# 80 instead of 64 gathered tokens, U products of 304 columns, and half scores and the last modulation in the step list of a transformer block with product-key experts

## The chip, the cores and the metric

The kernel runs on one core of a Trainium2 chip. The metric is device time in microseconds (us) of one execution, without compiling and without moving the inputs in; the median of three runs of the kernel before is 1428.74 us.

The engines named below: PE multiplies matrices (its weight loads are shown as PEld), DVE and ACT work on vectors, POOL does some vector work and issues gathers, SP issues most other transfers. Each engine takes its own instructions in the order in which they were written to its queue; semaphores hold one back until what it needs is there.

## The reference

512 tokens of width 1024 go through two mixers side by side (attention with a window of 128, and gated linear attention), an output projection, and then a layer of 16,384 experts. Each token picks, for each of 8 heads, 16 experts; an expert is one row of `u` and one row of `v`.

```python
def peer_ffn(h, wq, subkeys, u, v):
    q = (h @ wq).reshape(B, S, PEER_HEADS, 2, PEER_QDIM // 2)
    sub_scores = jnp.einsum('bshpk,hpnk->bshpn', q, subkeys)      # 2 x 128 scores a head
    top_v, top_i = lax.top_k(sub_scores, 16)
    cand = top_v[..., 0, :, None] + top_v[..., 1, None, :]        # 256 candidates
    cand_i = top_i[..., 0, :, None] * 128 + top_i[..., 1, None, :]
    best_v, best_pos = lax.top_k(cand, 16)
    expert = jnp.take_along_axis(cand_i, best_pos, axis=-1)
    gates = jax.nn.softmax(best_v, axis=-1)
    # per token, over its 8 x 16 experts:
    hid = gelu(einsum('tkd,td->tk', u[expert], h)) * gates
    return einsum('tk,tkd->td', hid, v[expert])

mod = silu(c) @ w_ada + b_ada                   # six vectors of 1024
shift1, scale1, gate1, shift2, scale2, gate2 = split(mod)
h = rms_norm(x, norm1_w) * (1 + scale1) + shift1
x = x + gate1 * (concat([attention(h), gla(h)]) @ w_out)
h2 = rms_norm(x, norm2_w) * (1 + scale2) + shift2
x = x + gate2 * peer_ffn(h2, wq, subkeys, u, v)
return rms_norm(x, final_norm_w)
```

## The kernel before

All products of 32-bit numbers are made of three matmuls on a high and a low part (`mm3`, L97 to L100); the high part is a copy by ACT (L91), the low one a subtraction, mostly by DVE (L92). The tokens stand in four blocks of 128.

**Front (0 to about 262 us).** Modulation, first norm, mixers, output projection, second norm. The work is written as generators, one step at a time; the list `parts` holds them, and the table `ORDER` (L49 to L66) names at each place the generator that makes its next step. All five engines follow this order by hand. `query_load` and `query_part` at its end make the query products of heads 0 and 1, in halves of 256 tokens. Vectors 3 and 4 of the modulation are steps of the list too.

**Query stage (262 to 396 us).** `wq_head(h)` (L1281) for h = 0 to 7: for h > 1 the query products (512 columns), then the scores `pss` of each pair of blocks (L1303), their copy by ACT, and on DVE the search for the 16 best of 128 by `max`, `max_index` and `match_replace` (L1314 to L1318). After heads 3 and 7 `candidates` (L1260) does the second search. Here also stands vector 5 of the modulation (`mod_part(5)` at h = 4; eight operations `macc` on DVE, L258 and L260) and the first chunks of the next stage as filler.

**Routing stage (396 to 732 us).** Two strands. One, on PE: the products `ph` of chunks of 128 experts' rows of u with h2 of the first 320 tokens (24 matmuls of 320 columns a chunk, `u_matmuls`, L1222), with a split of the chunk on ACT and DVE ahead and a GELU (L1229) behind; 86 of the 128 chunks are done here (`AHEAD`), the rest in the next stage. A chunk's split waits for the GELU of the chunk four earlier (`issue_after(gelus[-4])` in `u_part`). The other strand, on DVE above all: the routing itself (`route_heads`, `route`), then for 384 tokens, 16 at a time, the one-hot matrices that turn the gates into a dense table (`one_hot`, `gate_group`, L1450, L1468, L1471, with matmuls `pg` at L1483).

**The gathered tokens.** For the last 64 of these 384 tokens nothing is multiplied densely in U: their h2 is laid out in two copies on the partitions (`sp_rows`), their experts' numbers and gates are moved so that a partition holds one token's half (`sp_index`, L1541), and then POOL gathers 64 times 128 rows of u (`sp_gather`, L1562, 512 KB each) and DVE forms 128 dot products at a time (`sp_dot`, L1568). The rows turn through buffers: the first 20 (`HEAD`) through 7, the others through 3. Dot m frees its buffer and gather m + 3 is issued after it. `woven` places the 44 rows after the head among 51 pieces of the one-hot work. `sp_finish` applies GELU and `sp_close` multiplies by the gates and moves the result back.

What stands where on DVE and POOL is set by a planner: it sums DVE and PE work by a table of costs and takes the next U chunk when PE has fallen behind its share (`DVE_ALL`, `PE_ALL`). This stage holds a manual schedule on DVE and POOL, so the order that the planner writes is the order of execution.

**V stage (740 to 1402 us).** For 128 chunks: the dense table of gates times the GELU, times the rows of v, in `acc` (18 matmuls of 512 columns a chunk), with the 42 U chunks that are left between them; beside it POOL and DVE treat the fourth block's 128 tokens by gathered rows of u and v (`gather_u`, `gather_v`, L1618 to L1658). After it the final norm and the stores, to 1425.8.

Of the kernel before, what the change touches and what calls it, by code (L numbers as in the profile page):

```python
# [2156 lines left out]
```

## Time and profile before

| what | us |
|---|---|
| median of three runs (1428.49 to 1429.4) | 1428.74 |
| the profiled execution, its own time | 1427.61 |
| its span in the profile | 1425.8 |
| PE busy in the span | 1387.3 (97%) |
| DVE busy in the span | 1264.4 (89%) |
| ACT, POOL busy | 658.8, 608.2 |
| HBM read and written | 395.52 MB and 42.47 MB |

A page row gives for each engine its busy time and its number of instructions. The slices are the span in 40 equal parts, a digit the tenths in which an engine was busy. A window row gives busy times of the engines between two moments. A group row is one line of the code with one shape: how often, busy time, mean of one in ns, and the idle time ahead of them with what ended it. `his` and `los` are the high and low parts, `spr` the gathered rows, `spix` and `spg` their numbers and gates, `qsc` scores, `best` the results of a search, `macc` a sum of the modulation, `o` one-hot matrices.

### The profile page before, as it was taken

The numbers are of one execution on the slowest core, as the hardware profiler recorded it, in microseconds if no ns is written. First come the engines' busy times: TensorE is split into PE (matmuls) and PEld (weight loads), VectorE is DVE, ScalarE is ACT, GpSimd is POOL, SyncE is SP. The second block draws the span as 40 slices with busy tenths as digits, with TensorE's granted clock in tenths as the row PEclk, the third lists the DMA queues.
The fourth block names the chain that finished last, engine by engine and source line by source line (L and its number), as shares of the span: only waits on it lengthen the run. The fifth ranks groups of instructions, "written<-read, shape, count | busy, mean of one in ns | idle before, by whom it ended". The sixth has DMA issues, their size and how long they took to land.

```text
span 1425.8 us, 23257 instructions
## 1 busy us (share of the span) xinstructions
PE 1387.3 (97%) x8788; PEld 1224.4 (86%) x8788; DVE 1264.4 (89%) x2314; ACT 658.8 (46%) x1113; POOL 608.2 (43%) x400
## 2 busy tenths in 40 slices
PE   5999999999999999999989999999999999999997
PEld 4777788987999999999989888888888888888885
DVE  7778887599999999999978899999898998998986
ACT  4458565532444576666854333333333333333333
POOL 2000000334606444233145676767676776555510
PEclk9999999999999999999999999999999999999999
DMA  9621553352359999999889999999999999999962
GB/s 356 255 89 60 177 209 142 115 218 90 126 194 383 353 338 364 329 340 344 307 324 414 413 413 411 411 413 410 402 406 396 397 376 413 399 414 408 414 240 74
DMA packets 127873, 439.62 MB, mean 308 GB/s; under 512 B 11888, under 2 KB 48528, under 8 KB 107408
## 3 DMA queue, kind: packets, MB, share of 16 engines
q1 hardware_dynamic: 69024, 252.21, 46.4%
q0 software_dynamic: 47136, 171.99, 30.8%
q10 hardware_dynamic: 11600, 13.93, 2.7%
q8 instruction: 69, 1.13, 0.3%
q14 instruction: 44, 0.36, 0.1%
HBM read 395.52 MB, written 42.47 MB: 307 GB/s over the span
## 4 chain that ended last, share of the span: by engine, by line
PE 65%; DVE 6%; issue 6%; POOL 3%; DMA 1%; ACT 1%; ACTq 0%; POOLq 0%; DVEq 0%
PE acc L98 12%; PE acc L100 12%; PE acc L99 12%; PE ph L100 8%; PE ph L98 8%; PE ph L99 8%; POOL spr L1562 3%; PE pg L1483 2%; DMA spr<-in_u_dram,spix 1%; PE pq L99 1%; DVE macc L260 1%; PE pq L100 1%; PE pq L98 1%; DVE best L1315 1%; DVE qsc L1316 1%
## 5 line engine op out<-in xcount | busy, mean ns | idle before, releaser
L98 PE MATMUL ph<-h2Th,his 128*128 128x320 f32 x1024 | 319.7, 312 | 2.4 <-ACT his L1923 1.9
L100 PE MATMUL ph<-h2Th,los 128*128 128x320 f32 x1024 | 316.0, 310 | 2.5 <-DVE los L1930 1.8
L99 PE MATMUL ph<-h2Tl,his 128*128 128x320 f32 x1024 | 315.8, 308 | 0.0
L1618 POOL DMA_INDIRECT gu<-in_u_dram,ix_u x128 | 214.4, 1675 | 148.0 <-DVE gu L1628 82.4
L1653 POOL DMA_INDIRECT gv<-in_vP_dram,ix_v x128 | 210.5, 1644 | 111.9 <-DVE gacc L1658 86.9
L98 PEld LDWEIGHTS ph<-h2Th,his 128*128 128x128 f32 x1024 | 192.6, 188 | 4.3 <-ACT his L1923 2.1
L100 PEld LDWEIGHTS ph<-h2Th,los 128*128 128x128 f32 x1024 | 192.3, 188 | 3.5 <-DVE los L1930 2.0
L99 PEld LDWEIGHTS ph<-h2Tl,his 128*128 128x128 f32 x1024 | 192.7, 188 | 0.8
L1562 POOL DMA_INDIRECT spr<-in_u_dram,spix x64 | 104.8, 1637 | 170.9 <-DVE spr L1568 128.5
L98 PE MATMUL acc<-his,Ah 128*128 128x512 f32 x432 | 168.0, 389 | 0.0
L99 PE MATMUL acc<-los,Ah 128*128 128x512 f32 x432 | 168.0, 389 | 0.0
L100 PE MATMUL acc<-his,Al 128*128 128x512 f32 x432 | 168.0, 389 | 0.0
L1658 DVE SCALAR_TENSOR_TENSOR gacc<-gv,hg,gacc 128x1024 f32<-128x1024 f32 x127 | 162.5, 1280 | 3.2 <-DMA gv<-in_vP_dram,ix_v 3.0
L1628 DVE SCALAR_TENSOR_TENSOR gu<-gu,h2n 128x1024 f32<-128x1024 f32 x128 | 155.5, 1218 | 4.4 <-DMA gu<-in_u_dram,ix_u 4.4
L98 PE MATMUL acc<-hi,Ah 128*128 128x512 f32 x336 | 131.3, 391 | 0.0
L100 PE MATMUL acc<-hi,Al 128*128 128x512 f32 x336 | 131.1, 390 | 0.0
L99 PE MATMUL acc<-lo,Ah 128*128 128x512 f32 x336 | 130.7, 389 | 0.0
L1926 ACT ACTIVATE Ah<-gr 128x768 fp32r<-128x768 f32 x64 | 53.5, 836 | 139.8 <-PE acc L99 128.5
L91 ACT ACTIVATE his<-u 128x1024 fp32r<-128x1024 f32 x86 | 90.4, 1054 | 26.3 <-PE pq L99 11.6
L92 DVE TENSOR_TENSOR los<-u,his 128x1024 fp32r<-128x1024 f32 x75 | 91.2, 1218 | 5.5 <-ACT his L91 5.5
L98 PEld LDWEIGHTS acc<-his,Ah 128*128 128x128 f32 x432 | 81.1, 188 | 16.9
L100 PEld LDWEIGHTS acc<-his,Al 128*128 128x128 f32 x432 | 81.1, 188 | 16.8
(708 smaller groups left out, 2863.7 us busy)
## 6 DMA issues: line engine op xcount, KB each, us to landing
u<-in_uT_dram SPq DMA_DIRECT2D x43, 1024.0 KB, 7.5
gr<-Gd SPq DMA_DIRECT2D x15, 1536.0 KB, 11.1
Gd<-gs SPq DMA_DIRECT2D x10, 2048.0 KB, 10.0
gsp<-ge ACTq DMA_DIRECT2D x40, 320.0 KB, 6.4
wa<-in_w_ada_dram SPq DMA_DIRECT2D x12, 1024.0 KB, 5.3
wq<-in_wq_dram SPq DMA_DIRECT2D x8, 1024.0 KB, 5.7
gp<-gsp SPq DMA_DIRECT2D x22, 320.0 KB, 9.5
gp<-gsp SPq DMA_DIRECT2D x36, 160.0 KB, 9.6
```

The source lines that it names most:

```text
L91: nc.scalar.activation(hi, src, AF.Copy)
L92: lo_eng.tensor_tensor(lo, src, hi, OP.subtract)
L98: nc.tensor.matmul(acc, lh, rh, start=start, stop=False)
L99: nc.tensor.matmul(acc, lh, rl, start=False, stop=False)
L100: return nc.tensor.matmul(acc, ll, rh, start=False, stop=stop)
L1483: nc.tensor.matmul(pt[:, i, :], o12[:, g, 0, :, r], o2[:, g, m, :, r], start=(m == 0), stop=(m == 2))
L1562: nc.gpsimd.indirect_dma_start(out=sp[m], out_offset=None, in_=a["u"], in_offset=bass.IndirectOffsetOnAxis(ap=sp["ix", i][:, j:j + 1], axi ...
L1618: nc.gpsimd.indirect_dma_start(out=ur, out_offset=None, in_=a["u"], in_offset=bass.IndirectOffsetOnAxis(ap=ix_u[:, s:s + 1], axis=0))
L1628: nc.vector.scalar_tensor_tensor(ur, ur, 1.0, h2n, op0=OP.mult, op1=OP.mult, accum_out=hid[:, s:s + 1])
L1653: nc.gpsimd.indirect_dma_start(out=vr, out_offset=None, in_=a["vP"], in_offset=bass.IndirectOffsetOnAxis(ap=ix_v[:, s:s + 1], axis=0))
L1658: nc.vector.scalar_tensor_tensor(gacc, vr, hg[:, s:s + 1], gacc, op0=OP.mult, op1=OP.add)
L1926: nc.scalar.activation(grp(Ah), A, AF.Copy)
```

## The change

- `SETS` gets a second set: 16 tokens ahead of the 64. 80 tokens are gathered and dotted (80 rows instead of 64, the first set's rows with 8 copies of 16 tokens on the partitions), and the dense U products have 304 columns instead of 320.
- Two more groups in `ODD_AHEAD`, with two chunks each: 90 chunks are done in the routing stage instead of 86, and 38 in the V stage instead of 42.
- `woven` may take more than one row at a place (`while` for `if`), so 60 rows after the head stand at the same 51 places. The first set is finished in the first block of the one-hot work, the second where the one set was.
- `sp_index` and `sp_close` move each set with one transfer a copy: 8 of 16x16 for the first, 2 of 64x64 for the second.
- Vector 5 of the modulation is a generator of the step list; `query_part(h)` there makes the products of the first 256 tokens alone and their scores (`pssa`). `first_heads` then does, in an order by hand, the other 256 tokens' products of heads 0 and 1, their scores and the searches; `wq_head` serves h from 2 to 7. The two U chunks that stood after head 1 move to the others.
- `ORDER` is another table throughout (its other lines are left out below).

```diff
--- before.py
+++ after.py
...
-SETS = ((TD - 64, 64),)
+SETS = ((TD - 80, 16), (TD - 64, 64))
 TS = sum(n for c, n in SETS)
...
-ODD_AHEAD = tuple(range(21, 32))
+ODD_AHEAD = tuple(range(19, 32))
 KEPT = 3
...
ORDER = """
-2 2 2 2 2 0 0 0 0 2 0 2 0 0 0 2 25 25 0 0 2 13 0 13 13 25 25 25 13 0 1 1 1 1 2 1 13 1 1 25 25 2 13 25 1 2 13 25
...
+2 2 2 2 2 13 13 13 2 0 2 13 0 0 0 0 0 2 0 13 25 25 2 66 0 13 2 25 13 0 2 13 13 25 2 13 0 0 25 3 25 25 25 0 1 22
...
-                acc = Eg[:, 2 * v - 2:2 * v, :].rearrange("p a b -> p (a b)")
+                at = 4 if v == 3 else 6
+                acc = Eg[:, at:at + 2, :].rearrange("p a b -> p (a b)")
...
-    def query_part(h, half):
+    early = {}
+
+    def query_products(h, half):
         ts = slice(half * 256, half * 256 + 256)
         for s in range(2):
             for k in range(KD):
-                tag = "ph" if h == 0 else "m"
                 yield
-                if half == k == 0:
-                    query_banks[h, s] = pbank(f"pq{h}{s}") if h == 0 else bank(f"pq{h}{s}")
+                if half == s == k == 0:
+                    query_banks[h] = [pbank(f"pq{h}{i}") if h == 0 else bank(f"pq{h}{i}") for i in range(2)]
                 hh, ll = (t[:, s * P:(s + 1) * P] for t in queries[h, k])
-                mm3(query_banks[h, s][:, ts], hh, ll, h2Th[:, k, ts], h2Tl[:, k, ts], k == 0, k == KD - 1)
+                mm3(query_banks[h][s][:, ts], hh, ll, h2Th[:, k, ts], h2Tl[:, k, ts], k == 0, k == KD - 1)
+
+    def score_products(pt, qh, sk):
+        pt = pt.rearrange("p (a b c) -> p a b c", a=2, b=2)
+        for i in range(2):
+            for s in range(2):
+                nc.tensor.matmul(pt[:, i, s, :], qh[:, s, i * P:(i + 1) * P], sk[:, s, :], start=True, stop=True)
+
+    def query_part(h):
+        steps = query_products(h, 0)
+        next(steps)
+        for i in range(2 * KD):
+            yield
+            next(steps, None)
+        yield
+        if "q" not in early:
+            early["q"] = frW.tile([P, 2, 2, 256], F32, tag="h2_0", bufs=1, name="qh_")
+        for s in range(2):
+            nc.scalar.activation(early["q"][:, h, s], query_banks[h][s][:, :256], AF.Copy)
+        yield
+        if h == 0:
+            early["two"] = bank2("pssa")
+        score_products(early["two"][:, h], early["q"][:, h], early["sk", h])
...
-                 + [query_load(0), query_load(1)] + [query_part(h, half) for h in range(2) for half in range(2)]
-                 + [modulation(3), modulation(4)] + [attention_parts(n) for n in ALL])
+                 + [query_load(0), query_load(1)] + [query_part(h) for h in range(2)]
+                 + [modulation(3), modulation(4)] + [attention_parts(n) for n in ALL] + [modulation(5)])
...
+    def first_heads():
+        copy = lambda t, src: nc.scalar.activation(t, src, AF.Copy)
+        place = lambda pair: sca[:, pair].rearrange("p a b c -> p (a b c)")
+        for h in range(2):
+            nc.sync.dma_start(SKR[h], a["skT"][:, 2 * h:2 * h + 2, :])
+        rest = [query_products(h, 1) for h in range(2)]
+        for g in rest:
+            next(g)
+        run = lambda h, n: [next(rest[h], None) for _ in range(n)]
+        two = early.pop("two")
+        copy(place(0), two[:, 0])
+        copy(place(1), two[:, 1])
+        del two
+        run(0, 2 * KD)
+        search(0, 0, 0)
+        for s in range(2):
+            copy(qha[:, 0, s, 256:], query_banks[0][s][:, 256:])
+        run(1, KD)
+        two = bank2("pssb")
+        score_products(two[:, 0], qha[:, 0, :, 256:], SKR[0])
+        search(1, 0, 1)
+        copy(place(0), two[:, 0])
+        run(1, KD)
+        search(0, 1, 0)
+        for s in range(2):
+            copy(qha[:, 1, s, 256:], query_banks[1][s][:, 256:])
+        query_banks.clear()
+        return two
...
     def wq_head(h):
-        if h > 1:
-            w = load_group(a["wq"][h], h, 256, "wq", (nc.gpsimd, nc.gpsimd))
+        w = load_group(a["wq"][h], h, 256, "wq", (nc.gpsimd, nc.gpsimd))
...
-        for n0 in range(0, NT, 2):
-            pt = two[:, n0 // 2].rearrange("p (a b c) -> p a b c", a=2, b=2)
...
-                if h % 4 == 3:
+        for pair in range(2):
+            score_products(two[:, pair], qh[:, :, pair * 256:pair * 256 + 256], sk)
+            nc.scalar.activation(sca[:, pair].rearrange("p a b c -> p (a b c)"), two[:, pair], AF.Copy)
+            search(h, pair, pair)
+            if h % 4 == 3:
+                for n in range(2 * pair, 2 * pair + 2):
...
-        for src, key, dt in ((sp["e"], "ix", I32), (gates[SB], "g", F32)):
-            if i == 0:
-                for r in range(P // n):
-                    nc.sync.dma_start(sp[key, i][r * n:(r + 1) * n], src[s0:s0 + n, r * n:(r + 1) * n])
-            else:
-                d = dr.tile([P // n, n, n], dt, name=f"d{key}{i}")
-                nc.sync.dma_start(d.rearrange("r t j -> t r j"), src[s0:s0 + n].rearrange("t (r j) -> t r j", j=n))
-                nc.sync.dma_start(sp[key, i], d.rearrange("r t j -> (r t) j"))
+        for src, key in ((sp["e"], "ix"), (gates[SB], "g")):
+            for r in range(P // n):
+                nc.sync.dma_start(sp[key, i][r * n:(r + 1) * n], src[s0:s0 + n, r * n:(r + 1) * n])
...
+    engines = {mybir.EngineType.PE, mybir.EngineType.Activation, mybir.EngineType.DVE}
+    with tc.manual_schedule(engines=engines):
+        two = first_heads()
+    fetch(a["wq"][2], 2, 256, "wq")
+    score_products(two[:, 1], qha[:, 1, :, 256:], SKR[1])
+    nc.scalar.activation(sca[:, 1].rearrange("p a b c -> p (a b c)"), two[:, 1], AF.Copy)
+    search(1, 1, 1)
+    del two
+    for h in range(2, 8):
         wq_head(h)
-        if h == 1:
-            u_ahead(1, nc.vector)
-            u_ahead(2, nc.gpsimd)
...
-        if h == 4:
-            mod_part(5, gp, "gr", GR, bank2("mt5")[:, 0])
...
-                    if TS - len(rows) < HEAD + woven.place * (TS - HEAD) / 51:
+                    while rows and TS - len(rows) < HEAD + woven.place * (TS - HEAD) / 51:
...
-    head = (route(SB), sp_index(0), sp_rows(0), between(route(0), (0, 0, 1)), gate_transposes(0), between(route(1), (3, 3, 3)),
+    head = (route(SB), sp_index(0), sp_index(1), sp_rows(0), sp_rows(1), between(route(0), (0, 0, 1)), gate_transposes(0), between(route(1), (3, 3, 3)),
             between(gate_parts(0), (3,)), between(gate_rest(0), (3,)), between(iter([(0, 0)] * 2), (2, 2)))
-    first_block = {3: [gate_transposes(1)], 5: [gate_parts(1)], 6: [gate_rest(1)]}
+    first_block = {1: [sp_finish(0)], 2: [sp_close(0)], 3: [gate_transposes(1)], 5: [gate_parts(1)], 6: [gate_rest(1)]}
     second_block = {1: [route(GB)], 2: [gathered_index()], 6: [gate_transposes(SB, P // 2)], 7: [gate_parts(SB, 0, P // 2)]}
     second_block[7].append(first_place())
-    third_block = {0: [sp_finish(0)], 1: [sp_close(0), first_gates()], 2: [gate_turn(SB, P // 2, P)],
+    third_block = {0: [sp_finish(1)], 1: [sp_close(1), first_gates()], 2: [gate_turn(SB, P // 2, P)],
```

The order of DVE's queue in the middle of the routing stage (L1568, in the changed kernel L1613, is a dot of gathered rows; L92 a chunk's split; L1450, L1468, L1471, there L1500, L1518, L1521, one-hot work). Before:

```order
L1568 SCALAR_TENSOR_TENSOR spr,sphid_4383<-spr,xs_4399 128x1024
L1450 TENSOR_TENSOR o_028_5434<-iot,t_4552 128x2048
L1468 TENSOR_TENSOR o_030_5436<-o_024_5370,gp_4559 128x4x512
L1568 SCALAR_TENSOR_TENSOR spr,sphid_4383<-spr,xs_4399 128x1024
L92 TENSOR_TENSOR los<-u_5476,his 128x1024
L1450 TENSOR_TENSOR o_032_5507<-iot,t_4552 128x2048
L1568 SCALAR_TENSOR_TENSOR spr,sphid_4383<-spr,xs_4399 128x1024
L92 TENSOR_TENSOR los<-u_5476,his 128x1024
L1468 TENSOR_TENSOR o_038_5540<-o_028_5434,gp_4559 128x4x512
L1471 TENSOR_TENSOR o_038_5540<-o_028_5434,gp_4560 128x4x256
L1568 SCALAR_TENSOR_TENSOR spr,sphid_4383<-spr,xs_4399 128x1024
```

The same place of DVE's queue in the changed kernel:

```order
L1613 SCALAR_TENSOR_TENSOR spr,sphid_4423<-spr,xs_4445 128x1024
L1500 TENSOR_TENSOR o_032_5569<-iot,t_4598 128x2048
L92 TENSOR_TENSOR los<-u_5487,his 128x1024
L1613 SCALAR_TENSOR_TENSOR spr,sphid_4423<-spr,xs_4445 128x1024
L1518 TENSOR_TENSOR o_038_5602<-o_028_5527,gp_4605 128x4x512
L1521 TENSOR_TENSOR o_038_5602<-o_028_5527,gp_4606 128x4x256
L1613 SCALAR_TENSOR_TENSOR spr,sphid_4423<-spr,xs_4445 128x1024
L92 TENSOR_TENSOR los<-u_5635,his 128x1024
L1613 SCALAR_TENSOR_TENSOR spr,sphid_4423<-spr,xs_4445 128x1024
L1500 TENSOR_TENSOR o_036_5683<-iot,t_4598 128x2048
```

Between two dots stood two or three operations; now there are one or two.

The order of DVE's queue where the searches begin (L1314 to L1318, in the changed kernel L1313 to L1320, are a search; L258 and L260 vector 5 of the modulation; L1211 is there the last step of the second norm). Before, in the second search of head 0:

```order
L1316 MATCH_REPLACE qsc<-best,qsc 128x128
L1315 MAX_INDEX best<-best,qsc 128x8 x2
L1317 MAX best<-qsc 128x8 x2
L258 TENSOR_SCALAR macc_3311<-wa_0_3312,scs 128x1024
L1318 MAX_INDEX best<-best,qsc 128x8 x2
L260 SCALAR_TENSOR_TENSOR macc_3311<-wa_0_3312,scs,macc_3311 128x1024
L1316 MATCH_REPLACE qsc<-best,qsc 128x128 x2
L1314 MAX best<-qsc 128x8 x4
```

In the changed kernel, the norm's end and the first search:

```order
L1211 TENSOR_TENSOR h2Tl<-h_123_2391,h2Th 128x8x128
L1313 MAX best<-qsc 128x8 x2
L1315 MAX_INDEX best<-best,qsc 128x8
L1316 MATCH_REPLACE qsc<-best,qsc 128x128
L1315 MAX_INDEX best<-best,qsc 128x8
L1316 MATCH_REPLACE qsc<-best,qsc 128x128
L1318 MAX best<-qsc 128x8 x2
```

The modulation's operations no longer stand among the searches.

The order of SP's queue where the indices are moved (L1541, in the changed kernel L1590; L1220, there L1246, loads a chunk of u). Before:

```order
L1541 DMA spg_4382<-g 64x64 x2
L1220 DMA u_4449<-in_uT_dram 128x2048
L1220 DMA u_4521<-in_uT_dram 128x2048
L1541 DMA spix_4381<-spe 64x64 x2
L1220 DMA u_4604<-in_uT_dram 128x2048
```

The same place of SP's queue in the changed kernel:

```order
L1590 DMA spg_4394<-g 16x16 x8
L1590 DMA spg_4422<-g 64x64 x2
L1246 DMA u_4495<-in_uT_dram 128x2048
L1246 DMA u_4567<-in_uT_dram 128x2048
L1590 DMA spix_4393<-spe 16x16 x8
L1590 DMA spix_4421<-spe 64x64 x2
L1246 DMA u_4650<-in_uT_dram 128x2048
```

Ten moves stand where two stood, in each of the two places, with the same loads of u about them.

More of the change, by code (lines that the diff above doesn't have):

```diff
@@ L1093, in query_load @@
         nc.sync.dma_start(w, a["wq"][h])
+        early["sk", h] = frW.tile([P, 2, P], F32, tag="sk", bufs=2, name=f"sk{h}")
+        nc.sync.dma_start(early["sk", h], a["skT"][:, 2 * h:2 * h + 2, :])
         for half in range(2):
@@ L1162, in norm_half @@
             if n == 0:
-                h2s[n] = frW.tile([P, KD, P], F32, name="h2_0")
+                h2s[n] = frW.tile([P, KD, P], F32, tag="h2_0", bufs=1, name="h2_0")
             else:
@@ L1186, in norm_end @@
         if n == GB:
-            yield
-            two = bank2("h2n")
-            for k in range(KD):
-                nc.tensor.transpose(two[:, k // 4, k % 4 * P:(k % 4 + 1) * P], h2s[n][:, k, :], ident)
-            yield
-            for half in range(2):
-                nc.scalar.activation(h2n[:, half * 512:(half + 1) * 512], two[:, half], AF.Copy)
-            two = None
+            for half, tag in enumerate(("pt", "po")):
+                yield
+                pt = bank(f"h2n{half}", tag)
+                for i in range(4):
+                    nc.tensor.transpose(pt[:, i * P:(i + 1) * P], h2s[n][:, 4 * half + i, :], ident)
+                yield
+                nc.scalar.activation(h2n[:, half * 512:(half + 1) * 512], pt, AF.Copy)
+                pt = None
     with tc.manual_schedule(engines={mybir.EngineType.PE, mybir.EngineType.Activation, mybir.EngineType.DVE,
@@ L1279, in candidates, with search @@
             nc.vector.max_index(bp[:, h, 8:16], bv[:, h, 8:16], cb)
+    def search(h, pair, at):
+        ops = []
+        for i in range(2):
+            n = 2 * pair + i
+            both = [(TV[n][:, 2 * h + s, :], TI[n][:, 2 * h + s, :], sca[:, at, i, s, :], SC2[s]) for s in range(2)]
+            for v, ix, src, sc2 in both:
+                nc.vector.max(v[:, 0:8], src)
+            for v, ix, src, sc2 in both:
+                nc.vector.max_index(ix[:, 0:8], v[:, 0:8], src)
+                nc.vector.match_replace(sc2, v[:, 0:8], src, FMIN)
+            for v, ix, src, sc2 in both:
+                nc.vector.max(v[:, 8:16], sc2)
+            for v, ix, src, sc2 in both:
+                nc.vector.max_index(ix[:, 8:16], v[:, 8:16], sc2)
+    def first_heads():
[26 more added lines that the diff above has]
+        return two
     def wq_head(h):
-        if h > 1:
-            w = load_group(a["wq"][h], h, 256, "wq", (nc.gpsimd, nc.gpsimd))
+        w = load_group(a["wq"][h], h, 256, "wq", (nc.gpsimd, nc.gpsimd))
         qh = qha[:, h % 2]
@@ L1286, in wq_head @@
         nc.sync.dma_start(sk, a["skT"][:, 2 * h:2 * h + 2, :])
[L1287 to L1290 removed]
+        pq = [bank(f"pq{h}{s}", "m" if h % 2 else ("pt", "po")[s]) for s in range(2)]
         for s in range(2):
[L1292 to L1296 removed]
+            for k in range(KD):
+                hh, ll = w(k)
+                mm3(pq[s], hh[:, s * P:(s + 1) * P], ll[:, s * P:(s + 1) * P], h2Th[:, k, :], h2Tl[:, k, :], k == 0,
+                    k == KD - 1)
             nc.scalar.activation(qh[:, s, :], pq[s], AF.Copy)
         two = bank2(f"pss{h}")
[L1299 to L1319 removed]
+        for pair in range(2):
[4 more added lines that the diff above has]
+                for n in range(2 * pair, 2 * pair + 2):
                     candidates(n, h - 3, 4)
@@ L1519, in sp_rows @@
         nc.vector.tensor_tensor(w, rows(h2Th), rows(h2Tl), OP.add)
-        xs = rt.tile([P, D], F32, name="xs0") if i == 0 else gp.tile([P, D], F32, tag="gr", bufs=GR, name=f"xs{i}")
+        xs = rt.tile([P, D], F32, name="xs0") if n == 64 else gp.tile([P, D], F32, tag="gr", bufs=GR, name=f"xs{i}")
         for half in range(2):
@@ L1592, in sp_close @@
         nc.vector.tensor_tensor(hd, hd, sp["g", i], OP.mult)
-        if i == 0:
-            for r in range(P // n):
-                nc.sync.dma_start(gates[SB][s0:s0 + n, r * n:(r + 1) * n], hd[r * n:(r + 1) * n])
-        else:
-            d = dr.tile([P // n, n, n], F32, name=f"dhid{i}")
-            nc.sync.dma_start(d.rearrange("r t j -> (r t) j"), hd)
-            nc.sync.dma_start(gates[SB][s0:s0 + n].rearrange("t (r j) -> t r j", j=n), d.rearrange("r t j -> t r j"))
+        for r in range(P // n):
+            nc.sync.dma_start(gates[SB][s0:s0 + n, r * n:(r + 1) * n], hd[r * n:(r + 1) * n])
         yield 0.2, 0
@@ L1700, in peer_block_kernel @@
     WQ_U, LAST_U, LEAD_U, UCOST = 12, 2, 4.0, 24 * (TU / 2400 + 0.0133)
-    for h in range(8):
+    engines = {mybir.EngineType.PE, mybir.EngineType.Activation, mybir.EngineType.DVE}
[7 more added lines that the diff above has]
+    for h in range(2, 8):
         wq_head(h)
-        if h == 1:
-            u_ahead(1, nc.vector)
-            u_ahead(2, nc.gpsimd)
         if h == 2:
```

27 lines of the change are left out of this document (removed), and 30 rows, old and new, of the table ORDER.

## The prediction

> **What bounds the kernel now.** I read the page first (busy times and the span in slices), then windows by stage, then the groups of the routing stage, then the waits of the row gathers.
>
> ```profile
> PE 1387.3 (97%) x8788; PEld 1224.4 (86%) x8788; DVE 1264.4 (89%) x2314; ACT 658.8 (46%) x1113; POOL 608.2 (43%) x400
> PE   5999999999999999999989999999999999999997
> DVE  7778887599999999999978899999898998998986
> ```
>
> A slice is 35.6 us. PE is full almost everywhere, so the mean says little; DVE is full from slice 8 to slice 19 (some 285 to 713 us) and has room before and after. The stages apart, one row each (the second column is the length):
>
> ```profile
> core 0: us, PE busy (x) PEld busy (x) DVE busy (x) ACT busy (x) POOL busy (x), PEclk, DMA share, GB/s
> 262.00:396.00 134.00, 130.97 (x766) 117.68 (x765) 120.04 (x776) 50.33 (x71) 66.20 (x49) 0.99 0.40 144
> 396.00:490.00 94.00, 94.00 (x646) 93.98 (x645) 92.71 (x154) 40.98 (x66) 36.58 (x24) 1.00 0.82 313
> 490.00:680.00 190.00, 189.24 (x1749) 184.39 (x1748) 185.35 (x228) 130.15 (x292) 68.20 (x41) 1.00 0.94 340
> 680.00:732.00 52.00, 49.98 (x550) 47.89 (x549) 50.52 (x66) 43.20 (x111) 10.10 (x5) 1.00 0.83 290
> 740.00:1402.00 662.00, 660.24 (x3266) 571.70 (x3266) 598.76 (x622) 229.83 (x214) 413.17 (x249) 1.00 0.98 390
> 750.00:1000.00 250.00, 250.00 (x1289) 219.94 (x1289) 231.14 (x251) 89.36 (x86) 174.06 (x104) 1.00 1.02 412
> ```
>
> The query stage (262 to 396) has both engines near full. The routing stage (396 to 732) has PE and DVE full together: DVE works 92.71 + 185.35 + 50.52 = 328.6 of 336 us. The V stage (740 to 1402) is PE's: 660.24 of 662, with the transfers close behind (share 0.98, and 1.02 at 412 GB/s in its first part). So time leaves the V stage by less PE work, and the routing stage only by less work on both engines, or comes by more on either.
>
> **The change part by part.** All sums go against the profiled execution, 1427.61 us (span 1425.8, so 1.8 around it); the median of the runs is 1428.74, 1.1 above it.
>
> *1. V stage: fewer and narrower U products.* Here are the ends of two chunks' GELUs with PE alone behind them, and one stretch of 512-column products:
>
> ```profile
> 390.11 0.44 ACT L1229 ACTIVATE ge<-ph 128x320 f32<-128x320 f32 x1 [2.22 <-PE ph L100]
> 393.63 0.44 ACT L1229 ACTIVATE ge<-ph 128x320 f32<-128x320 f32 x1 [2.13 <-PE ph L100]
> 1260.00:1340.00 80.00, 80.00 (x355) 66.24 (x354) 0.00 (x0) 1.00 1.02 411
> ```
>
> A chunk of 24 products of 320 columns takes 3.52 us, 146.7 ns each; 512 columns take 80/355 = 225.4 ns. The slope is 0.41 ns a column, so 304 columns take about 140.1 ns (an estimate). The V stage's chunks fall from 42 to 38: 42 x 3.52 = 147.8 us becomes 38 x 24 x 0.1401 = 127.8. **-20.0 us**; PE never idles there, so it all counts unless transfers take over (rival B).
>
> *2. Routing stage: more work for DVE.* Each gathered row costs a dot on DVE, each chunk computed ahead a split:
>
> ```profile
> 442.81 1.21 DVE L1568 SCALAR_TENSOR_TENSOR spr<-spr,xs 128x1024 f32<-128x1024 f32 x1
> 443.96 1.21 DVE L92 TENSOR_TENSOR los<-u,his 128x1024 fp32r<-128x1024 f32 x1
> 445.10 1.21 DVE L1568 SCALAR_TENSOR_TENSOR spr<-spr,xs 128x1024 f32<-128x1024 f32 x1
> L1568 DVE SCALAR_TENSOR_TENSOR spr<-spr,xs 128x1024 f32<-128x1024 f32 x64 | 77.5, 1216 | 5.5 <-DMA spr<-in_u_dram,spix 5.5
> L92 DVE TENSOR_TENSOR los<-u,his 128x1024 fp32r<-128x1024 f32 x74 | 89.9, 1217 | 0.0
> ```
>
> Successive starts lie 1.15 and 1.14 us apart (busy times overlap a little). 16 more dots and 4 more splits, and the second set's sum of h2 (one more operation of that size): 21 x 1.14 = **+24 us**. DVE has nothing else to give up here, the number of gate groups stays 24, so it counts whole. PE's own work hardly changes: its 4 added chunks (13.4 us) cost what 80 narrower chunks save (80 x 24 x 6.6 ns = 12.7), so PE will now wait for DVE.
>
> *3. The ring of gathered rows.* The first 20 rows turn through 7 slots, the rest through 3; a row's gather is issued when the dot three before it has freed its slot, and DVE takes instructions in order, so a late row stops everything behind its dot: splits, hence PE, and the one-hot gates.
>
> ```profile
> L1562 POOL DMA_INDIRECT spr<-in_u_dram,spix x64: 937/1682/2028, 427.4 to 666.5; - x64
>   DVE spr L1568: 128.5, 45
>   DMA spix<-spe: 34.9, 1
>   DMA spr<-in_u_dram,spix: 5.5, 6
> DMA to landing us min/median/max: 5.3/8.9/14.6
> ...
> 427.44 2.03 POOL L1562 DMA_INDIRECT spr<-in_u_dram,spix  x1 [34.86 <-DMA spix<-spe]
> 429.76 1.83 POOL L1562 DMA_INDIRECT spr<-in_u_dram,spix  x1 [0.30 <-issue]
> 487.54 1.22 DVE L1568 SCALAR_TENSOR_TENSOR spr<-spr,xs 128x1024 f32<-128x1024 f32 x1
> 679.19 1.21 DVE L1568 SCALAR_TENSOR_TENSOR spr<-spr,xs 128x1024 f32<-128x1024 f32 x1
> ```
>
> A turn needs 0.3 us for the issue and 8.9 for the landing: 9.2. Dots 20 to 63 (the last two rows: first and last of them) lie (679.19 - 487.54)/43 = 4.46 us apart; three of these less a dot's 1.15 leave 12.2 us for a turn, and DVE waited for a row only 5.5 us in all. Afterwards 60 rows share the same places: the other work in that stretch is 191.7 - 43 x 1.15 = 142 us, plus 59 dots of 1.15 is 210, or 3.56 us a row; a turn then leaves 9.5 us. The mean is just enough, but the dots are not evenly spread (see the order: two pieces, then one). Summing the durations between dots in the new order, 22 of 57 turns leave under 9.2 us and the shortest 6.3; the shortfalls add up to 31 us. A wait at one dot also lengthens the next two turns, so a third to a half of it is paid: 12 to 23 us, against 5.5 before. Bounds: about 0 more, if rows land within 6.3 us (5.3 is the fastest seen), and 31 less 5.5. I take 17.5 in all, **+12 us**, since the median landing is the nearest row. Beside this row a page of the Trainium skill speaks for less: "DMA: Bandwidth & Descriptors", section "Anatomy of one DMA — SWDGE (gpsimd) path", fits a GpSimd transfer at 2.0 us plus its bytes over 436 GB/s, which gives an estimate of 3.2 us for 512 KB. By that rule the ring never waits and this term is nothing (the first rival's case); the 8.9 us measured beside other traffic disagrees with it.
>
> *4. Index moves.* The set of 16 tokens has its indices and gates moved by 8 transfers each, where one set had 2.
>
> ```profile
> 410.71 1.16 SPq L1541 DMA_DIRECT2D spg<-g  x2
> 423.91 1.11 SPq L1541 DMA_DIRECT2D spix<-spe  x2
> ```
>
> One issue takes 0.55 us, so the eighth lands 6 x 0.55 = 3.3 us later and with it the first gather. Some chunks' splits stand ahead of the first dot, which hides a part: **+2 us** (0 to 3.3). The eight on the way back lie beside gate work and cost nothing unless the gates of block 2 wait for them.
>
> *5. Routing begins earlier.* The last modulation leaves DVE's queue in the query stage, and half of heads 0 and 1 is scored from the stepped part:
>
> ```profile
> L260 DVE SCALAR_TENSOR_TENSOR macc<-wa,scs,macc 128x1024 f32<-128x1024 f32 x7 | 12.8, 1822 | 0.4 <-DMA wa<-in_w_ada_dram 0.4
> L258 DVE TENSOR_SCALAR macc<-wa,scs 128x1024 f32<-128x1024 f32 x1 | 2.5, 2505 | 0.0
> ...
> 270.54 0.28 PE L100 MATMUL pq<-h2Th,los 128*128 128x256 f32 x1
> 272.81 0.87 DVE L1314 MAX8 best<-qsc 128x8 f32<-128x128 f32 x4 [10.17 <-ACT qsc L1306]
> 373.18 1.05 PE L1303 MATMUL pss<-qsc 128*128 128x128 f32 x8
> 396.30 1.05 DVE L1336 TENSOR_TENSOR g<-best 128x512 f32<-128x512 f32 x1
> L1303 PE MATMUL pss<-qsc 128*128 128x128 f32 x128 | 17.7, 277 | 3.0 <-DVE modT L252 3.0
> ```
>
> DVE loses 15.3 us of work and starts its searches up to 9 or 10 us sooner (its idle of 10.17 us before 272.81). By DVE alone routing (396.30, the first operation of the gates) would start some 18 us earlier, leaving some waits. But PE is nearly as full. The halves of heads 0 and 1 left over now follow h2's end: I put their end at 274 (270.54 before), then 6 heads x 48 x 225.4 ns = 65, the scores 12 (112 of the 128; eight take 1.05 us with a last one of 0.28, so 0.11 each), and by the new order 2.2 U chunks of 3.36, 7: the last score at 358 to 360, against 374. Its searches and candidates end about 378. Then the splits that stand among the first routing operations wait for products: a split reuses buffers whose chunk, four earlier, must be done; the ninth chunk is done only 6.8 x 3.36 = 23 us behind the last score, at 382. Routing so runs as if it began at about 386: **-10 us** (bounds: 0, if PE is as late as before, and -18).
> The modulation's 8 operations in front (9 us at 1.15, up to the 15.3 they take now) fall where the DVE row shows 7 and 5 tenths busy (slices 6 and 7, some 28 us free); PE there loses 48 half products of 0.12 us. With the new step list I take 0 for the stepped part, and ±5.
>
> *6. Transfers in the V stage.* 390 GB/s x 662 us is 258 MB; 4 MB of u fewer in 642 us is 396 GB/s. The stretches at 412 GB/s and share 1.02 have no room: the narrower products give PE time back there that the transfers may not follow. **+2 us** (0 to 6).
>
> **Sum:** -20 + 24 + 12 + 2 - 10 + 2 = +10, so 1437.6, and with 1.1 to the median **1438 us**.
>
> **The rivals.**
> *A, faster.* Rows land in time. In favour: DVE waited 5.5 us before, POOL itself was free for 128.5 us, and landings as short as 5.3 us occur; against: the median of 8.9 with a margin of 0.3. It decides at a landing of some 7 us: term 3 is then 0, and if PE also doesn't hold routing up (term 5 at -18), the sum is -20 + 24 + 0 + 2 - 18 + 2 = -10: 1419. This is also what the quoted rule of the skill would give.
> *B, transfers bound the V stage.* For: share 1.02 at 412 GB/s for 250 us, and gu and gv gathers in the same queues. Against: PE idles nowhere there. If the V stage kept its 662 us but for half of the gain, +10 on the sum: 1448.
> *C, no change.* The ring waits as in term 3 but routing gains the whole 18 (sum +2), or the ring waits little and PE gives 10 (sum -2): 1427 to 1431.
> *D, that the edit doesn't reach the work:* the new order does hold 80 dots and 90 chunks; not weighed further.
>
> **How the numbers follow.** Forecast (1433 to 1443) and what lies about it 0.47, A 0.22 (1416 to 1426), B 0.13 (1443 to 1452), C 0.18 (1426 to 1432). 8 in 10 lie in 1418 to 1449: it takes in the ring's two bounds one at a time, not with everything else at its end. The forecast's own range is 1432 to 1445. A measurement of this kernel tells 0.2% (2.9 us) from no change: faster 0.22, within 0.2% 0.18, slower 0.60.
>
> **What would show it.** Right: in the V stage PE full and about 20 us shorter; in the routing stage 24 us more DVE work, DVE's wait for gathered rows 15 to 25 us in 12 or more waits, PE idle 30 us or more between the routing's start and the last gate (now 2.8 us), routing's first operation by 380 to 388. Wrong: DVE's wait for rows still about 5 us (A); PE idle or weight loads waiting on DMA in the V stage (B); routing's start before 380 with splits not waiting for products, or a stepped part that ends more than 5 us from 262.

## The result: 1438.8 us, 0.65% slower, and where the time went

| | before | after |
|---|---|---|
| median of the runs, us | 1428.62 (4 runs, 1428.04 to 1429.4) | 1438.83 (4 runs, 1435.9 to 1439.88) |
| the profiled execution, own time and span | 1427.61, 1425.8 | 1435.9, 1434.0 |
| ratio, 95% interval | | 1.0065 (1.0049 to 1.0081) |

The profiled execution of the changed kernel is the fastest of its four, so differences of profiles come out some 2 us smaller than those of medians: +8.2 us between the spans, +10.2 between the medians. Kernels with the same front differ by as much ahead of the first search: the second norm's first `h2Tl` starts at 234.4 us in the changed kernel and at 237.4 in experiment 3. So a single profile tells starts to about 3 us; lengths of the same stage agree better (98.8 to 100.7 us for one first part below).

The page of the changed kernel: busy times and slices.

```profile
PE 1373.4 (96%) x8796; PEld 1207.4 (84%) x8796; DVE 1274.5 (89%) x2349; ACT 660.1 (46%) x1122; POOL 628.1 (44%) x417
PE   6999999999999989899898999999999999999997
DVE  7768888679899999899996899999999989899997
```

PE has lost 14 us of work and now shows 8 tenths in some slices of the routing stage (14, 16, 19 and 21, counted from 0); the time went where PE waits. I cut both kernels where the same operations start: the first operation of the routing (`g` on DVE), the 21st dot of gathered rows, the last one-hot matmul `pg`, the high part of the V stage's first chunk, and the V stage's last matmul `acc` (the last three columns are PE's clock, the share of the transfer engines and GB/s). Before:

```profile
396.30:487.50 91.20, 91.20 (x627) 91.18 (x626) 89.91 (x148) 38.18 (x62) 35.62 (x23) 1.00 0.82 315
487.50:730.90 243.40, 240.61 (x2307) 233.76 (x2305) 237.27 (x297) 174.78 (x403) 79.26 (x46) 1.00 0.91 328
737.60:1415.80 678.20, 674.59 (x3328) 583.44 (x3328) 610.43 (x647) 236.45 (x230) 413.17 (x249) 1.00 0.96 385
```

After:

```profile
381.40:480.50 99.10, 95.20 (x672) 93.43 (x671) 91.30 (x148) 43.38 (x70) 37.70 (x24) 0.98 0.79 300
480.50:759.40 278.90, 254.15 (x2398) 243.62 (x2397) 262.23 (x334) 176.85 (x410) 102.65 (x62) 0.98 0.92 327
765.80:1423.10 657.30, 653.36 (x3232) 562.33 (x3232) 601.35 (x645) 232.40 (x224) 408.54 (x250) 0.99 0.98 394
```

Routing starts 14.9 us earlier (381.4 for 396.3). Its first part takes 7.9 us longer, its second 35.5, the V stage 20.9 less: -14.9 + 7.9 + 35.5 - 20.9 = +7.6, and the span grew by 8.2. In the second part DVE has 262.2 us of work for 237.3, and PE, which had 2.8 us free, has 24.8.

What DVE waited for in the changed kernel's routing stage (the sum, the number of times and the longest):

```profile
DVE spr L1613 <- DMA spr<-in_u_dram,spix: 17.3, 16, 3.0
DVE los L92 <- ACT his L91: 5.7, 3, 3.4
```

And the landing of its gathered rows, from the answer on that tile:

```profile
DMA to landing us min/median/max: 5.0/8.5/11.5
```

DVE stands 17.3 us at 16 late rows (5.5 us in 6 before). The landing itself has not become slower (8.5 us, 8.9 before): the rows are late because each has less time.

### The profile page after: what moved, and what is told of

The parts are those of the page before. It is cut to its first block, busy times and chain, and to the rows that moved or that the text cites. A ratio compares the mean times of both kernels' runs of the same rounds, so it can differ in the third digit from the quotient of the medians.

```text
span 1434.0 us, 23419 instructions
## 1 busy us (share of the span) xinstructions
PE 1373.4 (96%) x8796; PEld 1207.4 (84%) x8796; DVE 1274.5 (89%) x2349; ACT 660.1 (46%) x1122; POOL 628.1 (44%) x417
## 4 chain that ended last, share of the span: by engine, by line
PE 59%; issue 12%; DVE 11%; DMA 8%; POOL 7%; ACT 1%; POOLq 0%; ACTq 0%; SPq 0%; DVEq 0%
PE acc L100 9%; PE acc L98 9%; PE acc L99 9%; POOL spr L1607 7%; PE ph L100 4%; PE ph L98 4%; PE ph L99 4%; DMA gu<-in_u_dram,ix_u 3%; PE pq L100 2%; PE pq L99 2%; PE pq L98 2%; DMA spr<-in_u_dram,spix 1%; DMA gv<-in_vP_dram,ix_v 1%; DVE o L1500 1%; DVE los L92 1%
## 5 line engine op out<-in xcount | busy, mean ns | idle before, releaser
L100 PE MATMUL ph<-h2Th,los 128*128 128x304 f32 x1024 | 313.8, 308 | 15.9 <-DVE los L92 13.9
L98 PE MATMUL ph<-h2Th,his 128*128 128x304 f32 x1024 | 316.6, 309 | 10.8 <-ACT ge L1255 9.0
L99 PE MATMUL ph<-h2Tl,his 128*128 128x304 f32 x1024 | 311.1, 304 | 0.0
L1607 POOL DMA_INDIRECT spr<-in_u_dram,spix x80 | 130.7, 1634 | 189.4 <-DVE spr L1613 139.1
L1668 DVE SCALAR_TENSOR_TENSOR gu<-gu,h2n 128x1024 f32<-128x1024 f32 x128 | 155.2, 1216 | 24.8 <-DMA gu<-in_u_dram,ix_u 24.8
L100 PE MATMUL acc<-his,Al 128*128 128x512 f32 x444 | 172.8, 389 | 0.3 <-DVE Al L1980 0.3
L98 PE MATMUL acc<-his,Ah 128*128 128x512 f32 x444 | 172.8, 389 | 0.0
L99 PE MATMUL acc<-los,Ah 128*128 128x512 f32 x444 | 172.7, 389 | 0.0
L98 PE MATMUL acc<-hi,Ah 128*128 128x512 f32 x324 | 126.3, 390 | 0.0
L100 PE MATMUL acc<-hi,Al 128*128 128x512 f32 x324 | 126.2, 390 | 0.0
L1613 DVE SCALAR_TENSOR_TENSOR spr<-spr,xs 128x1024 f32<-128x1024 f32 x80 | 97.1, 1218 | 17.7 <-DMA spr<-in_u_dram,spix 17.3
L92 DVE TENSOR_TENSOR los<-u,his 128x1024 fp32r<-128x1024 f32 x78 | 94.9, 1218 | 5.7 <-ACT his L91 5.7
```

The costliest lines, as they stand in the source:

```text
L92: lo_eng.tensor_tensor(lo, src, hi, OP.subtract)
L98: nc.tensor.matmul(acc, lh, rh, start=start, stop=False)
L99: nc.tensor.matmul(acc, lh, rl, start=False, stop=False)
L100: return nc.tensor.matmul(acc, ll, rh, start=False, stop=stop)
L1607: nc.gpsimd.indirect_dma_start(out=sp[m], out_offset=None, in_=a["u"], in_offset=bass.IndirectOffsetOnAxis(ap=sp["ix", i][:, j:j + 1], axi ...
L1613: nc.vector.scalar_tensor_tensor(r, r, 1.0, sp["x", i], op0=OP.mult, op1=OP.mult, accum_out=sp["hid", i][:, j:j + 1])
```

## The experiments

All ratios are against the kernel before, whose median in the three groups of runs was 1427.99, 1428.87 and 1427.56 us.

The stretches of every run, from its own profile, cut at the same operations:

```
                              routing   to the    21st dot to   V stage's
                              starts    21st dot  last one-hot  length      median us
before                        396.3      91.2       243.4        678.2       1428.6
the change                    381.4      99.1       278.9        657.3       1438.8
1 step list part alone        382.5      97.2       245.6        679.3       1423.1
2 80 rows alone               394.1      93.2       280.5        656.8       1444.6
3 four buffers                384.4      98.8       269.6        657.5       1424.7
4 short first dots            383.9     100.0       278.0        656.9       1438.1
5 86 chunks ahead             383.4      99.7       275.9        670.0       1448.6
6 four buffers, short dots    382.9     100.7       267.2        657.0       1423.3
7 four buffers, 94 ahead      383.8     100.5       271.4        653.6       1425.8
8 four buffers, 98 ahead      382.5     106.3       270.8        653.1       1430.9
9 no late gathers             383.5      99.2       261.7        658.0       1418.8
10 no late gathers, short     382.9      99.3       247.8        655.7       1405.1
11 step list, four buffers    382.9      97.2       244.0        678.8       1421.1
12 94 ahead, fewer v gathers  381.6     100.5       269.1        642.3       1412.8
```

### 1 and 2: the two halves of the change

Experiment 1 takes the gathered tokens back and keeps the step list, the half scores and the moved modulation:

```diff
-SETS = ((TD - 80, 16), (TD - 64, 64))
+SETS = ((TD - 64, 64),)
...
-ODD_AHEAD = tuple(range(19, 32))
+ODD_AHEAD = tuple(range(21, 32))
...
```

> The changed kernel with 64 gathered tokens, products of 320 columns and 86 chunks ahead as before; what stays of the change is the step list, the half scores and the moved modulation. Theory (term 5 of the prediction, with PE as the second bound): DVE starts the routing near 381 us as in the changed kernel, but PE was idle only some 7 us between 262 and 738 us, so the V stage starts 4 to 7 us earlier and the time is 1421 to 1425. Rival (the terms simply add): 1418 or less. Rival (the earlier start is worth nothing): 1428.

Experiment 2 is the kernel before with the opposite edit, and `sp_index`, `sp_close`, `woven` and the places of the sets as in the change:

```diff
-SETS = ((TD - 64, 64),)
+SETS = ((TD - 80, 16), (TD - 64, 64))
...
-ODD_AHEAD = tuple(range(21, 32))
+ODD_AHEAD = tuple(range(19, 32))
...
```

> The kernel before with 80 gathered tokens, products of 304 columns and 90 chunks ahead alone; step list, scores and modulation as before. Theory: 26 us more DVE work and some 12 us more waiting for rows in the routing stage, 21 us less in the V stage: 1428.6 + 17 to 19 = 1445 to 1448, with a DVE wait for rows of 15 to 20 us. Rival (rows land in time as before): 5 us of such waits and 1434 to 1436.

Measured: 1423.14 us (0.9963, 0.995 to 0.9975) and 1444.63 us (1.0122, 1.01 to 1.0144). The step list part is a gain of 4.9 us, the rows part a loss of 16.6; together 11.8, and the change measured 10.2. Experiment 1 lies where the theory with PE as second bound put it, and experiment 2 just under its range (1445), with a wait for rows of 18.8 us as its theory had it. Experiment 1's routing stage in its two parts:

```profile
382.50:479.70 97.20, 96.85 (x664) 96.56 (x662) 91.26 (x148) 40.48 (x64) 36.67 (x24) 1.00 0.81 311
479.70:725.30 245.60, 242.66 (x2317) 235.16 (x2315) 237.33 (x297) 175.12 (x404) 79.16 (x46) 1.00 0.92 325
```

PE is full in both. The 13.8 us by which routing starts sooner lose 6.0 at once: PE is busy for the whole of the first part and makes 664 matmuls in it, where it made 627 before. The rows part alone (experiment 2) adds 2.0 us to the first part (93.2 for 91.2) and the change over experiment 1 adds 1.9 (99.1 for 97.2). The first set's index moves stand there: in experiment 2 the first gather goes out 34.8 us after the routing's start (428.9 less 394.1), before it was 31.1 (427.4 less 396.3).

### 3 and 4: the ring, and the dots before it

Experiment 3 gives the rows after the first 20 a fourth buffer:

```diff
-        k = m % 7 if m < HEAD else m % 3
+        k = m % 7 if m < HEAD else m % 4
...
+            sp["r4"] = gp.tile([P, D], F32, tag="gr", bufs=GR, name="spr4")
...
-        while sp_dot.next < min(TS, m + 8 if sp_dot.next < HEAD else m + 4):
+        while sp_dot.next < min(TS, m + 8 if sp_dot.next < HEAD else m + 5):
```

> The changed kernel with 4 buffers instead of 3 for the rows after the first 20 (the fourth is one of the gathers' buffers that stand empty then). Theory: DVE's wait for rows falls from 17.3 us to 4 or less, the V stage starts 12 to 14 us earlier, 1425 to 1428. Rival (the rows are late because transfers are slow together, more in flight only land later): landing rises from 8.5 to 11 us or more and the time stays within 1434 to 1439.

Experiment 4 shortens the first set's 16 dots:

```diff
+        if i == 0:
+            nc.vector.scalar_tensor_tensor(r[:, :2], r[:, :2], 1.0, sp["x", i][:, :2], op0=OP.mult, op1=OP.mult,
+                                           accum_out=sp["hid", i][:, j:j + 1])
+        else:
...
```

> The changed kernel in which the 16 dots of the first set read 2 columns instead of 1024 (their sums are left out, everything is still gathered). Theory (DVE's work sets the length of the routing stage): 16 x 1.07 = 17 us less DVE work, V stage 15 to 17 us earlier, 1422 to 1424. Rival (the first rows' landing or PE sets it there): under half of it, 1431 or more.

Measured: 1424.71 us (0.9967, 0.9953 to 0.9981) for the fourth buffer. Its gathered rows:

```profile
  DMA spr<-in_u_dram,spix: 1.5, 2
DMA to landing us min/median/max: 5.3/9.1/12.9
```

And its later part:

```profile
483.20:752.80 269.60, 250.42 (x2401) 240.55 (x2399) 261.22 (x335) 177.50 (x410) 103.48 (x61) 0.99 0.93 337
```

The wait is gone (1.5 us) at a landing of 9.1 us, and the time is 14.1 us under the change's. The rival, rows landing later when more are under way, is out. In the stretch the gain shows as 9.3 us (278.9 to 269.6); the two profiled executions themselves lie only 7.3 us apart (experiment 3's is its slowest run, 1428.6, the change's its fastest, 1435.9).

Experiment 4 is a miss: 1438.12 us (1.0074, 1.0052 to 1.0096), no gain at all. The part ahead of the 21st dot:

```profile
383.90:483.90 100.00, 96.19 (x682) 94.64 (x681) 75.16 (x148) 44.15 (x72) 30.36 (x24) 0.98 0.79 301
```

Its waits for the first set's rows:

```profile
DVE spr L1614 <- DMA spr<-in_u_dram,spix: 12.4, 8, 3.8
```

DVE works 75.2 us of 100 instead of 91.3 of 99.1 and the part is not shorter. Its freed 16 us went into waiting: 12.4 us for these 16 rows and 3.9 for the next ones, where the changed kernel waited 1.7 us for rows in this part. PE is busy 96.2 us of it. I had put the bound of this part on DVE; with less DVE work, DVE stands for rows instead, and PE, nearly full, would leave at most 4 us. Which of these two is the nearer bound was not taken apart. The change's 16 more dots stand in the later part (20 dots ahead of the 21st in both kernels), so this experiment tested the wrong place.

### 6, 9 and 10: dots and transfers behind the 21st dot

Experiment 6 is experiment 3 with every fourth later dot, 15 of 60, on 2 columns:

```diff
+        w = 2 if m >= HEAD and m % 4 == 3 else D
-        nc.vector.scalar_tensor_tensor(r, r, 1.0, sp["x", i], op0=OP.mult, op1=OP.mult,
+        nc.vector.scalar_tensor_tensor(r[:, :w], r[:, :w], 1.0, sp["x", i][:, :w], op0=OP.mult, op1=OP.mult,
```

> As with 4 buffers, but every fourth dot behind the 20th (15 of 60) reads 2 columns (its sums are left out). Theory: from the 20th row to the last one-hot work DVE sets the pace, so 15 x 1.07 = 16 us less work there shorten that stretch from 270 by 12 to 16 us, 1409 to 1413 in all; a limit is PE, busy 250 of these 270 us. Rival (as with the first set's short dots, rows or products set the pace there too): under 6 us, 1419 or more.

A second miss: 1423.31 us (0.9954, 0.993 to 0.9978), 1.4 us under experiment 3 (1.9 by the two ratios), the rival's number. The intervals of the two ratios allow anything from 2 us slower to 6 us faster, all of it short of the theory's 12 to 16. Its later part:

```profile
483.60:750.80 267.20, 249.71 (x2388) 242.92 (x2386) 247.03 (x335) 175.80 (x404) 97.42 (x61) 0.97 0.92 340
```

And the waits there:

```profile
ACT his L91 <- DMA u<-in_uT_dram: 19.0, 5, 4.8
PE ph L98 <- ACT ge L1255: 13.7, 6, 5.3
DVE los L92 <- ACT his L91: 11.9, 4, 5.9
```

DVE now has 20 us free and PE 17, and neither sets the pace alone: ACT waits 19.0 us for chunks of u, and behind that in its queue stand the high parts for DVE's splits and the GELUs for which PE waits. The loads of u run beside the gathers, at 340 GB/s and a share of 0.92. So "DVE is full, hence its work counts whole" could be wrong in two ways: DVE is no bound, or it is one of two with the same length. Experiments 9 and 10 tell these apart. Experiment 9 (three buffers again) issues no gathers from row 23 on and multiplies the dots from row 20 on by zero, and 10 shortens 15 dots as well:

```diff
+        if m >= HEAD + 3:
+            return
         nc.gpsimd.indirect_dma_start(out=sp[m], out_offset=None, in_=a["u"],
...
```

> The changed kernel without the gathers of rows 23 to 79 (their dots read what lies in the buffers, times zero): no waiting for rows, and some 30 MB less to move in the routing stage; all dots stay. Theory (behind the waits for rows, transfers and DVE bound that stretch together): hardly better than with 4 buffers, 1420 to 1425, the stretch from the 20th dot to the last one-hot work 262 to 268 us. Rival (transfers alone are what holds it with 4 buffers): stretch near PE's 250 us, 1407 to 1412.

> The same, and every fourth dot behind the 20th (15 of 60) on 2 columns. Theory (two bounds together): with both the transfers and 16 us of DVE work gone the stretch falls to PE's 250 to 255 us, 1406 to 1412, though the DVE work alone gave 1.4 us with the gathers in place. Rival (DVE's work is not a bound at all): as without the gathers alone, within 3 us.

Measured: 1418.81 us (0.9926, 0.9903 to 0.9949) and 1405.11 us (0.9835, 0.9807 to 0.9862). Both lie about 1 us under their theories' ranges and far from the rivals (6.8 us and more). The later part in experiment 9, then in experiment 10:

```profile
482.70:744.40 261.70, 249.44 (x2397) 237.78 (x2396) 260.84 (x334) 176.82 (x409) 10.29 (x5) 1.00 0.68 234
```

```profile
482.20:730.00 247.80, 243.59 (x2396) 238.33 (x2395) 246.20 (x335) 176.41 (x409) 8.40 (x5) 0.99 0.72 249
```

And the wait for u in experiment 10:

```profile
ACT his L91 <- DMA u<-in_uT_dram: 2.6, 2, 1.5
```

The loads of u in that part (number, size, median time to landing), in experiment 6 and then in 10:

```profile
u<-in_uT_dram SPq DMA_DIRECT2D x24, 1024.0 KB, 11.1
u<-in_uT_dram SPq DMA_DIRECT2D x24, 1024.0 KB, 5.1
```

Without the gathers DVE is busy 260.8 of 261.7 us, and the 15 dots are then worth 13.7 us, where they gave less than 2 with the gathers. So both are bounds of nearly one length: with the gathers and short dots the part takes 267.2 us, with the dots and no gathers 261.7, with both 269.6, with neither 247.8. Leaving the gathers out takes POOL's issues away too; these were not separated from the transfers, but the wait for u (19.0 us in experiment 6, 2.6 in 10) and the landing of its loads (8.5 and 11.1 us in experiments 3 and 6, 5.5 and 5.1 in 9 and 10) point to the transfers.

### 5, 7, 8 and 12: chunks ahead, and the bound of the V stage

Only `ODD_AHEAD` differs: it begins at 21 in experiment 5 (86 chunks, three buffers), at 17 and 15 in 7 and 8 (94 and 98 chunks, four buffers). Here that of 7:

```diff
-ODD_AHEAD = tuple(range(19, 32))
+ODD_AHEAD = tuple(range(17, 32))
```

> The changed kernel with 86 chunks ahead instead of 90, so 42 of 304 columns left for the V stage. Theory: the V stage grows by 4 x 3.36 = 13.4 us, the routing stage, bound by DVE from the 20th row on, shrinks by the 4 splits, 4.6 us: 9 us more than the change, 1446 to 1449. Rival (the splits stand where rows are awaited anyway): 13 us more, 1451 to 1453. Rival (transfers bound the V stage, so PE work there is nearly free): under 4 us more.

> As with 4 buffers, with 94 chunks ahead. Theory: 13.4 us less in the V stage, 4.6 us more DVE work, and PE has some 19 us idle behind the 20th row: 1424.7 - 9 = 1414 to 1418. Rival (PE or loads of u become the bound in the routing stage): 1421 to 1425.

> As with 4 buffers, with 98 chunks ahead. Theory: a further 13.4 us less in the V stage, but 26.8 us of added products exceed the 19 us that PE had idle, so the second step brings less than the first: 1409 to 1416. Rival (PE or loads become the bound at the first step): 1421 or more.

Measured: 1448.59 us (1.0128, 1.0092 to 1.0164), as expected; 1425.77 (0.9969, 0.9953 to 0.9985) and 1430.87 (1.0005, 0.9991 to 1.0018), at or next to what the rivals of 7 and 8 said in the total (1421 to 1425, and 1421 or more), though at 94 chunks not for their reason: the routing stage grew by 3.5 us over experiment 3, less than the 4.6 forecast, and what failed to come is the gain in the V stage. Per four chunks taken out of it the V stage loses 12.7 us (670.0 to 657.3), then 3.9 (657.5 to 653.6), then 0.5. The V stage at 94 chunks:

```profile
761.90:1415.50 653.60, 642.58 (x3138) 548.58 (x3136) 598.85 (x644) 226.17 (x218) 403.99 (x250) 0.99 0.98 393
```

And DVE's waits in it:

```profile
DVE gacc L1700 <- DMA gv<-in_vP_dram,ix_v: 20.9, 25, 2.0
DVE gu L1670 <- DMA gu<-in_u_dram,ix_u: 20.2, 20, 2.3
```

DVE's waits in the V stage of the change itself, at 90 chunks:

```profile
DVE gu L1668 <- DMA gu<-in_u_dram,ix_u: 24.8, 17, 3.8
DVE gacc L1698 <- DMA gv<-in_vP_dram,ix_v: 17.9, 16, 2.6
```

Before, from the groups of the two lines:

```profile
L1628 DVE SCALAR_TENSOR_TENSOR gu<-gu,h2n 128x1024 f32<-128x1024 f32 x128 | 155.5, 1218 | 4.4 <-DMA gu<-in_u_dram,ix_u 4.4
L1658 DVE SCALAR_TENSOR_TENSOR gacc<-gv,hg,gacc 128x1024 f32<-128x1024 f32 x127 | 162.5, 1280 | 3.2 <-DMA gv<-in_vP_dram,ix_v 3.0
```

DVE waits for gathered rows some 41 to 43 us at 90 and at 94 chunks (7.4 us in the kernel before), but PE, free for 3.9 us at 90 chunks (653.36 of 657.3), now stands for 11.0 (653.6 less 642.58): the waits have reached it. Experiment 12 is experiment 7 with fewer gathers of v rows:

```diff
+        if s % 4 == 3:
+            vr = gather_v.last
...
```

> 94 chunks ahead with 4 buffers, with every fourth gather of v rows left out in the V stage (32 of 128; its sum takes the row before again): 17 MB less to move there, the same work on DVE and PE. Theory (with 94 chunks ahead transfers took over from PE, 653.6 us where PE's work alone would take 644): the V stage falls to 643 to 647, 1415 to 1419 in all. Rival (the V stage is held by DVE's work or by the copies of gates, not by transfers): 652 us or more, 1423 to 1426.

Measured: 1412.82 us (0.9888, 0.986 to 0.9917), 2 us under the theory's range, and its V stage 0.7 under. The V stage:

```profile
757.50:1399.80 642.30, 638.66 (x3136) 548.09 (x3136) 597.91 (x643) 225.56 (x218) 360.19 (x218) 1.00 0.94 374
```

And the larger of DVE's two waits for rows there:

```profile
DVE gu L1670 <- DMA gu<-in_u_dram,ix_u: 2.8, 3, 1.2
```

The landing of the rows of v, in experiment 7 and then in 12:

```profile
DMA to landing us min/median/max: 2.8/15.7/21.1
DMA to landing us min/median/max: 2.8/10.4/18.7
```

With 17 MB less to move, the same work on PE and DVE ends 11.3 us sooner, close to PE's own 638.7 busy. So what holds the V stage at 94 chunks is the gathers, and neither PE nor DVE. Fewer gathers also mean fewer issues on POOL and a slower turn of the buffers; these were not separated, but the shorter landing (15.7 to 10.4 us) speaks for the transfers. At 98 chunks the routing stage's first part grows as well (106.3 for 98.8 us, PE busy 103.2): there PE has no room for more chunks, as the rival of 8 said.

### 11: the step list part with four buffers

The edits of experiments 1 and 3 together.

> The step list, half scores and moved modulation alone (64 rows, 320 columns, 86 chunks ahead), with 4 buffers. Theory: DVE waited 7.4 us for rows there, but PE is full in the routing stage (346.2 of 349.5 us), so at most 3 us: 1420 to 1423. Rival (waits for rows cost their whole length): 1416 to 1418.

Measured: 1421.12 us (0.9948, 0.9929 to 0.9966), as PE's being full there let expect. It is the fastest kernel here that computes everything: 6.4 us under the kernel before. Against experiment 3 it also shows the rows part without the ring's waits: the 16 more rows and 4 more chunks lengthen the later routing part by 25.6 us (244.0 to 269.6) and shorten the V stage by 21.3 (678.8 to 657.5), a loss of some 3 us (3.6 by the medians, 2.7 by the ratios).

## Why the prediction was right, step by step

- **V stage, -20 us:** 20.9 (678.2 to 657.3). Four chunks are 12.7 of it by experiment 5, the narrower products the rest.
- **DVE's work, +24 us, counted whole:** the work came (in the part behind the 21st dot 262.2 for 237.3 us, +25), and so did its length: +25.6 between experiments 11 and 3, where hardly any wait for rows is left. But the reason was incomplete. The step that failed is "DVE has nothing else to give up here, so it counts whole": in the first part waits for rows took up what DVE's work gave free, beside a nearly full PE (experiment 4), and in the second the part takes almost the same time with 16 us less of it as long as the gathers run (experiment 6). The size came out because two bounds lie side by side; experiments 9 and 10 show it, in which DVE's work does count once the gathers are gone.
- **The ring, +12 us:** DVE's waits for rows went from 5.5 to 17.3 us (17.5 forecast), and the fourth buffer took 14.1 us off the changed kernel and 2.0 off experiment 1: 12.1 for the added waits. The condition given, 9.2 us needed against 9.5 on the mean and unevenly spread, stands. By the Trainium skill ("DMA: Bandwidth & Descriptors", section "Anatomy of one DMA — SWDGE (gpsimd) path") a row would land in 3.2 us, an estimate from its fit. The traces disagree: the landing's median was 8.2 to 10.6 us over the rows of each profile here, its least 4.8 to 6.2. The rival that followed that rule fell.
- **Index moves, +2 us:** 2.0, by experiment 2 against before, and again 1.9 by the change against experiment 1. With the same first part, profiles differ by up to 2 us in its length, so the size is rough.
- **Routing earlier, -10 us:** about half of it came. Routing starts 14.9 us earlier, but experiment 1, which has this part alone, is only 4.9 us faster: its first routing part is 6.0 us longer and its second 2.2. Over experiment 2 the change gains 5.8. The limit that the prediction named, a full PE, shows in experiment 1's first part. The waits at splits whose products are not done, by which it let the routing run as if begun at 386, were 2.3 us of DVE's 5.7; the other 3.4 lie behind ACT, which waited 3.6 us for the routing's own first operation and then loaded a table for 1.3.
- **Transfers in the V stage, +2 us:** nothing yet. The stage shrank by as much as PE's work; the limit lies just below, at 653 us (experiments 7 and 8). The rival named for it is true from 94 chunks on, not at 90.

The forecast was right to about 1 us, and that is in part luck. Taken by halves, the rows part was forecast at +20 us (-20 + 24 + 12 + 2 + 2) and measured at +16.6 (experiment 2) and +15.7 (the change over experiment 1); most of that difference is the V stage, 21.4 us shorter in experiment 2 where 18 had been forecast. The earlier routing was forecast at -10 and measured at -4.9 and -5.8. The two errors have opposite signs. One sign named as right was missed narrowly: PE was idle 28.7 us between the routing's start and the last gate (99.1 + 278.9 less 95.2 and 254.15), where 30 or more had been named. And one figure in the working is off, without weight for the sum: four chunks of u are 2 MB, not 4 (the V stage loads 21 pieces of 1 MB before and 19 after).

So the sign and the rough size follow from the trace of before. The V stage's products, the ring and the index moves held in size and reason; DVE's work was right in size beside a bound that the prediction had weighed for the V stage alone; the earlier routing brought half, and the transfers nothing.

## What to carry to other kernels

Work moved from a bound engine to a stage where another is "full" needs more than that engine's busy time: ask what would pace the stage if that work were free, and look at the transfers it brings with it, since here they held the stretch nearly as long as the dots did. A ring of buffers is checked by its short turns and not by the mean: at 3 buffers a mean margin of 0.3 us cost 14 us, and one more buffer of 512 KB, borrowed where it lay idle, gave it back. And a stage that loses work to another shrinks only down to its second bound, which four chunks more here were enough to reach.
